# An expert stage fed by a weight stream: units of four experts moved ahead of the units of two, early loads by halves, and the last unit's products split by a branch

## The chip, the cores and the metric

The kernel runs on one core of a Trainium2 chip. The metric is the device time of one launch in microseconds (us). Before the change the median of 3 runs is 766.7 us (766.11 to 768.42). For this kernel, a difference within about 0.3% (2.3 us) can't be told from none.

## The reference

One layer of a hybrid encoder block on 256 tokens of width 1024, batch 1, in f32:

```
mod = silu(c) @ w_ada + b_ada                      # shift, scale, gate, twice
h   = rms_norm(x) * (1 + scale1) + shift1
... = h @ w_in                                     # two token mixers: neighbourhood and latent attention
x   = x + gate1 * (merged @ w_out)
h2  = rms_norm(x) * (1 + scale2) + shift2
scores = sigmoid(h2 @ w_router)                    # 64 experts, the best 8 of each token, group-limited
a   = silu(h2 @ w_gate[e]) * (h2 @ w_up[e]) * gate[token, e]
x   = x + gate2 * (sum over e of a @ w_down[e] + shared expert)
```

Each of the 64 experts has a gate and an up matrix of 1024 x 256 and a down matrix of 256 x 1024, so 3 MB in f32. Every expert's weights are read from HBM once: some 200 MB, most of what the kernel moves.

## The kernel before

The first 290 us or so are the two token mixers and the router. What the change touches is the expert stage behind them.

**Ranks and units.** The router counts the tokens of each expert, and the kernel sorts the experts by that count on the chip. The sorted places are called ranks. A *unit* is a group of experts that is computed together in 128 columns: two experts with 64 token slots each, two with 96 and 32, or four with 32 each (`UNITS`, L45 to L48). There are 26 units; `SEQ` is the order in which the ranks are loaded and used, and the units use up 64 experts in that order. I write U0, U1, ... U25 for the units in the order in which they run. Before the change U0 to U2 are units of two, and then come three units of two and one of four, again and again: the units of four are U6, U10, U14, U18, U22 and U25.

**Slots.** The weights live in six slots `Sl` (gate and up, 2 MB each) and six slots `Dl` (down, 1 MB each; in the rows one of them is called bias_t, and S and D stand for the others). The expert that is loaded into a slot is the one six places later in `SEQ`, so a unit's loads can only start when the unit that used those slots is through with them: `load_gu` (L790) when the products with gate and up are done, `load_dn` (L794) when the products with down are done. All of these loads are issued by SyncE (SP), in program order. An expert's number is itself read from a table in SBUF by SP (L774).

**A unit on TensorE (PE).** `middle(U)` computes the products with gate and up for k = 0 to 7 (`gate_up`, L1192), and between them, for the unit before, the products that add its result to the tokens (`last`, which calls `combine`: L1244 and L1245, with an add on VectorE, L1246). Behind `middle` come the unit's SiLU (L1213, L1214), the slot matrix (L1201), a part of the gather of tokens for units to come (L1179), the transposes (L1218) and the products with down (L1226), whose results are scaled and split in two (L1231 to L1233). The four or two experts of a unit stand beside each other in the columns of the array, so that a unit of four has as much work on PE as a unit of two, and twice the weights.

**The branch.** `past_slots` (L1281, L1282) holds a branch: if some expert had more tokens than its slots, extra passes are made. PE, VectorE, ScalarE and SyncE each read the largest overflow from SBUF into a register and branch on it; with the given inputs all four jump over the body. It stands in `middle` of the last unit, U25, behind the `last` of U24 and ahead of U25's own products.

**The tail.** Behind the products of U25 come its SiLU, transposes and down products, then `last_out` and the final adds, and four stores of the result (L1453).

Of the kernel before, what the change touches and what calls it, by code (L numbers as in the profile page):

```python
# [24 lines left out]
KD = D // P  # L25
# [16 lines left out]
TWOS = [((r, r + 54), (96, 32)) for r in range(6, 10)] + [((r, r + 1), (64, 64)) for r in range(10, 36, 2)]  # L42
FOURS = [(tuple(range(r, r + 4)), (32,) * 4) for r in range(36, 60, 4)]

UNITS = [((r, r + 1), (64, 64)) for r in (0, 2, 4)]  # L45
for u in FOURS:
    UNITS += TWOS[:3] + [u]
    del TWOS[:3]  # L48
SEQ = [r for u in UNITS for r in u[0]]
NUN = len(UNITS)  # L50

# [18 lines left out]
def unit_at(U):  # L70

    return sum(len(u[0]) for u in UNITS[:U])
# [3 lines left out]
def kernel(ctx, tc, x, c, positions, w_ada, b_ada, g_norm1, w_in, g_na_q, g_na_k,  # L76
# [710 lines left out]
    def load_gu(i, js=(0, 1), ks=slice(0, 8)):  # L787
        if i <= E:
            for j in js:
                Y.dma_start(gu_w(i)[:, j, ks], weights(i)[j].rearrange("(p k) f -> p k f", k=KD)[:, ks])  # L790

    def load_dn(i):
        if i <= E:
            Y.dma_start(dn_w(i), weights(i)[2].rearrange("(j p) d -> p j d" if i == 0 else "(p j) d -> p j d", j=2))  # L794
# [95 lines left out]
    for b in range(KD):  # L890
        u = 10 + b // 2
# [240 lines left out]
    def unit_slot(U):  # L1132

        return U % 4, U % 2
# [49 lines left out]
    def group_dst(g):  # L1184
        s = 2 * (g % 2)
        return lambda k: xg[:, s:s + 2, k]

    def gate_up(p, slot, U, ks, at=None):
        at = unit_at(U) + 1 if at is None else at
        for k in ks:  # L1190
            for c, w, i, _ in unit_tiles(U):
                T.matmul(p[c:c + w], xg[:, slot, k, c:c + w], gu_w(at + i)[:, :, k],  # L1192
                         start=(k == 0), stop=(k == KD - 1))
# [18 lines left out]
    def act(p):  # L1212
        A.activation(a_, p[:, 0:FF], AF.Silu)  # L1213
        V.tensor_tensor(a_, a_, p[:, FF:2 * FF], op=ALU.mult)  # L1214

    def a_trans():
        for j in range(2):
            T.transpose(b_mi[:, j * 128:(j + 1) * 128], a_[:, j::2], ident)  # L1218
        V.tensor_copy(aT.rearrange("p j n -> p (j n)"), b_mi[:, :256])  # L1219

    def down_mm(U, hf, at=None):
        at = unit_at(U) + 1 if at is None else at
        p = r_yy()
        for j in range(2):
            for c, w, i, _ in unit_tiles(U):
                T.matmul(p[c:c + w], aT[:, j, c:c + w], dn_w(at + i)[:, j, hf * 512:hf * 512 + 512],  # L1226
                         start=(j == 0), stop=(j == 1))
        return p
# [6 lines left out]
    def down(U, side, at=None):  # L1235
        for hf in range(2):
            down_out(down_mm(U, hf, at), hf, side)

    def combine(side, t, hfs=range(2)):
        so = so_t(side, t)  # L1240
        for hf in hfs:
            n_ = slice(hf * 512, hf * 512 + 512)
            p = r_co()
            T.matmul(p, so, yHt[:, hf], start=True, stop=False)  # L1244
            T.matmul(p, so, yLt[:, hf], start=False, stop=True)  # L1245
            V.tensor_tensor(X[:, t, n_], X[:, t, n_], p, op=ALU.add)  # L1246
# [19 lines left out]
    def past_slots():  # L1266


        on = [ENG.PE, ENG.DVE, ENG.Activation, ENG.SP]

        def load(i, r):
            if r < NS:
                w = w_exp_gate[0, r], w_exp_up[0, r], w_exp_down[0, r]
            else:
                v = nc.values_load(ordi[0:1, r - NS:r - NS + 1], min_val=0, max_val=E - 1, engines=[ENG.SP])
                w = [w_[0, bass.ds(v, 1)].rearrange("o a b -> (o a) b") for w_ in (w_exp_gate, w_exp_up, w_exp_down)]
            for j in range(2):
                Y.dma_start(gu_w(i)[:, j], w[j].rearrange("(p k) f -> p k f", k=KD))
            Y.dma_start(dn_w(i), w[2].rearrange("(p j) d -> p j d", j=2))

        most = nc.values_load(cmax[0:1, E // 2:E // 2 + 1], min_val=0, max_val=S, engines=on)  # L1281
        with tc.If(most > 0):  # L1282
            for j, U in enumerate(PAIRS):
                nv = nc.values_load(cmax[0:1, j:j + 1], min_val=0, max_val=S, engines=on)
                with tc.If(nv > 0):
                    for i, r in enumerate(UNITS[U][0]):
                        load(free_at + i, r)
                    cap = CAPS[2 * j]
                    extra(U, cap)
                    with tc.If(nv > 64):  # L1290
                        for first in range(cap + 64, S, 64):
                            extra(U, first)
# [3 lines left out]
    def last_out(pd):  # L1296

        down_out(pd[0], 0, 1)
        V.scalar_tensor_tensor(yB, pd[1], gsl2[1], gate2[:, 512:], op0=ALU.mult, op1=ALU.mult)

    def middle(U, early=lambda: None, also=lambda: None):

        gu = lambda ks: gate_up(b_gu, unit_slot(U)[0], U, ks)
        g, r = U // 2, U % 2
        oh_n = oh2[(g + 1) % 2]

        def last(t):
            if U:
                combine((U - 1) % 2, t)

        if U + 1 == NUN:
            for t in range(NT):
                last(t)
            past_slots()
            gu(range(KD))
            act(b_gu)
            a_trans()
            last_out([down_mm(U, hf) for hf in range(2)])
            return
        gu(range(0, 2))  # L1320
        early()
        if r == 0 and g + 1 < NGRP:
            for z in range(2):
                one_hot(oh_n, U + 2 + z)
        gu(range(2, 3))
        last(0)
        gu(range(3, 5))
        last(1)
        gu(range(5, 8))
        also()  # L1330
# [86 lines left out]
    for U in range(NUN):  # L1417
        g, r = U // 2, U % 2
        more = g + 1 < NGRP
        oh_n = oh2[(g + 1) % 2]  # L1420
        middle(U, *([] if U else [by_ranks, first_side]))
        if U + 1 == NUN:
            break

        nxt = [unit_at(U) + i + 1 + NS for i in range(len(UNITS[U][0]))]
        for ks in ((slice(0, 4), slice(4, 8)) if U == 0 else (slice(0, 8),)):
            for i in nxt:
                load_gu(i, ks=ks)
        act(b_gu)
        if U == 0:  # L1430
            for t in range(NT):
                shared_down(t)
            load_dn(NS)
        slot_side(oh2[(U + 1) // 2 % 2], U + 1, (U + 1) % 2)
        pg = [gather_mm(oh_n, 0, 4, 2 * r)] if more else []
        a_trans()
        if more:
            pg.append(gather_mm(oh_n, 0, 4, 2 * r + 1))
        for i, p in enumerate(pg):
            gather(oh_n, 0, 4, group_dst(g + 1), 2 * r + i, p)  # L1440
        down(U, U % 2)
        for i in nxt:
            load_dn(i)
# [32 lines left out]
```

## Time and profile before

| what | value |
|---|---|
| median of 3 runs | 766.7 us |
| the profiled execution's own time | 766.27 us |
| its span, first to last instruction | 764.6 us |
| TensorE (PE) busy | 707.4 us, 93% of the span |
| VectorE (DVE) busy | 394.8 us, 52% |
| ScalarE (ACT) busy | 221.2 us, 29% |
| GpSimd (POOL) busy | 12.2 us, 2% |
| mean granted TensorE clock | 0.957 |
| moved by DMA | 259.92 MB, mean 340 GB/s |

The busy share of PE counts matmuls that are slowed by the low clock as fully busy, and most of a matmul's time in the expert stage is the streaming of weights through the array. The span is 1.7 us shorter than the execution's own time. The expert stage starts at about 286 us of the span (the first products of L1192) and goes on to its end.

### The profile page before, as it was taken

The numbers are of one execution on the slowest core, as the hardware profiler recorded it, in microseconds if no ns is written. First come the engines' busy times: TensorE is split into PE (matmuls) and PEld (weight loads), VectorE is DVE, ScalarE is ACT, GpSimd is POOL, SyncE is SP. The second block draws the span as 40 slices with busy tenths as digits, with TensorE's granted clock in tenths as the row PEclk, the third lists the DMA queues.
The fourth block names the chain that finished last, engine by engine and source line by source line (L and its number), as shares of the span: only waits on it lengthen the run. The fifth ranks groups of instructions, "written<-read, shape, count | busy, mean of one in ns | idle before, by whom it ended". The sixth has DMA issues, their size and how long they took to land. (4 is left out here: it accounts for less than half of the span.)

```text
span 764.6 us, 12045 instructions
## 1 busy us (share of the span) xinstructions
PE 707.4 (93%) x4577; PEld 416.4 (54%) x4577; DVE 394.8 (52%) x942; ACT 221.2 (29%) x423; POOL 12.2 (2%) x52
## 2 busy tenths in 40 slices
PE   5998999999999999999999979996999699959957
PEld 4886968788799984444444423441445144514423
DVE  4555786545587487555555434542455244424422
ACT  3334474546654532111221111121112112201200
POOL 5000000000000100000000000000000000000000
PEclk9999998999999999999999989997999799979969
DMA  9999953745877967799999999999999999999981
GB/s 281 351 365 317 272 166 111 238 149 165 293 256 285 354 259 266 305 407 401 393 387 423 420 421 420 422 420 420 421 421 421 420 421 420 421 421 421 420 368 57
DMA packets 82347, 259.92 MB, mean 340 GB/s; under 512 B 5197, under 2 KB 54375, under 8 KB 57961
## 3 DMA queue, kind: packets, MB, share of 16 engines
q1 hardware_dynamic: 77204, 254.32, 86.0%
q10 hardware_dynamic: 4628, 4.74, 1.9%
q8 instruction: 38, 0.62, 0.3%
q14 instruction: 29, 0.23, 0.1%
q0 software_dynamic: 448, 0.02, 0.1%
HBM read 258.00 MB, written 1.05 MB: 339 GB/s over the span
## 5 line engine op out<-in xcount | busy, mean ns | idle before, releaser
L1192 PE MATMUL B<-S,xg 128*32 128x512 f32 (+1 forms) x1152 | 217.2, 638 | 33.5 <-DMA S<-in_w_exp_up_dram 27.2
L1192 PEld LDWEIGHTS B<-S,xg 128*32 128x32 f32 (+1 forms) x1152 | 60.1, 126 | 158.0 <-issue 138.5
L1246 DVE TENSOR_TENSOR X<-X,B 128x512 f32<-128x512 f32 x102 | 65.6, 683 | 94.8 <-PE B L1245 94.8
L1226 PE MATMUL B<-D,bias_t 128*32 128x512 f32 (+1 forms) x488 | 94.9, 597 | 1.1 <-DVE bias_t L1219 1.1
L1213 ACT ACTIVATE bias_t<-B 128x256 f32<-128x256 f32 x26 | 10.0, 386 | 249.3 <-PE B L1192 249.3
L1231 DVE SCALAR_TENSOR_TENSOR bias_t<-B,bias_t,gate 128x512 f32<-128x512 f32 x51 | 38.3, 750 | 38.8 <-PE B L1226 36.2
L1232 ACT CAST yHt<-bias_t 128x512 fp32r<-128x512 f32 x51 | 31.5, 617 | 84.9 <-DVE bias_t L1231 84.9
L1179 PE MATMUL B<-oh,xnH 128*128 128x256 f32 x208 | 53.8, 292 | 0.4 <-ACT xg L1167 0.4
L1226 PEld LDWEIGHTS B<-D,bias_t 128*32 128x32 f32 (+1 forms) x488 | 26.8, 121 | 49.3 <-issue 43.6
L1233 DVE TENSOR_TENSOR yLt<-bias_t,yHt 128x512 fp32r<-128x512 f32 x51 | 35.3, 692 | 34.9 <-ACT yHt L1232 34.9
L1179 PE MATMUL B<-oh,xnL 128*128 128x256 f32 x208 | 51.7, 281 | 0.0
L1214 DVE TENSOR_TENSOR bias_t<-bias_t,B 128x256 f32<-128x256 f32 x26 | 10.9, 421 | 73.1 <-ACT bias_t L1213 73.1
L408 DVE TENSOR_TENSOR Rw<-D,Rw 128x1024 fp32r<-128x1024 f32 x34 | 40.8, 1221 | 13.8 <-ACT Rw L403 13.6
L1244 PE MATMUL B<-yHt,so 128*128 128x512 f32 x102 | 46.2, 453 | 1.1 <-ACT yHt L1232 1.0
L1244 PEld LDWEIGHTS B<-yHt,so 128*128 128x128 f32 x102 | 19.3, 189 | 47.9 <-issue 20.8
L1167 ACT ACTIVATE xg<-B,sh,G 128x256 f32<-128x256 f32 x52 | 29.0, 564 | 52.7 <-PE B L1179 41.5
L1245 PE MATMUL B<-yLt,so 128*128 128x512 f32 x102 | 41.0, 402 | 0.4 <-DVE yLt L1233 0.2
L1226 PE MATMUL B<-bias_t 128*64 128x512 f32 (+1 forms) x88 | 40.0, 597 | 0.0
L1179 PEld LDWEIGHTS B<-oh,xnH 128*128 128x128 f32 x208 | 39.5, 190 | 0.6 <-ACT xg L1167 0.6
L119 PE MATMUL B<-Rh,Rw 128*128 128x256 f32 x128 | 39.6, 309 | 0.0
L1179 PEld LDWEIGHTS B<-oh,xnL 128*128 128x128 f32 x208 | 39.3, 189 | 0.2 <-DVE xnL L1335 0.2
L120 PE MATMUL B<-Rh,Rw 128*128 128x256 f32 x128 | 37.1, 290 | 0.0
(365 smaller groups left out, 1154.3 us busy)
## 6 DMA issues: line engine op xcount, KB each, us to landing
S<-in_w_exp_up_dram SPq DMA_DIRECT2D x62, 1024.0 KB, 19.8
S<-in_w_exp_gate_dram SPq DMA_DIRECT2D x62, 1024.0 KB, 15.3
D<-in_w_exp_down_dram SPq DMA_DIRECT2D x53, 1024.0 KB, 19.7
S<-in_w_ada_dram SPq DMA_DIRECT2D x20, 1024.0 KB, 8.5
bias_t<-in_w_exp_down_dram SPq DMA_DIRECT2D x11, 1024.0 KB, 19.7
D<-in_w_in_dram SPq DMA_DIRECT2D x6, 1024.0 KB, 13.4
S<-in_w_ada_dram SPq DMA_DIRECT2D x8, 512.0 KB, 7.3
D<-in_w_in_dram SPq DMA_DIRECT2D x8, 512.0 KB, 8.4
```

Of the source, the lines that this page charges most:

```text
L119: T.matmul(p, a[0], b[0], start=first, stop=False)
L120: T.matmul(p, a[0], b[1], start=False, stop=False)
L408: V.tensor_tensor(w_st[u][:, 1, z_], Dl[u % 2][:, z_], w_st[u][:, 0, z_], op=ALU.subtract)
L1179: T.matmul(p[:, k2 * 256:k2 * 256 + w], part[:, t, k], oh[:, t, c0:c0 + n].rearrange("p a b -> p (a b)"), start=(i == 0), stop=(i == 3))
L1192: T.matmul(p[c:c + w], xg[:, slot, k, c:c + w], gu_w(at + i)[:, :, k], start=(k == 0), stop=(k == KD - 1))
L1226: T.matmul(p[c:c + w], aT[:, j, c:c + w], dn_w(at + i)[:, j, hf * 512:hf * 512 + 512], start=(j == 0), stop=(j == 1))
L1231: V.scalar_tensor_tensor(yF, p, gsl2[side], gate2[:, hf * 512:hf * 512 + 512], op0=ALU.mult, op1=ALU.mult)
L1232: A.copy(yHt[:, hf], yF)
L1233: V.tensor_tensor(yLt[:, hf], yF, yHt[:, hf], op=ALU.subtract)
L1244: T.matmul(p, so, yHt[:, hf], start=True, stop=False)
L1245: T.matmul(p, so, yLt[:, hf], start=False, stop=True)
L1246: V.tensor_tensor(X[:, t, n_], X[:, t, n_], p, op=ALU.add)
```

## The change

Three edits. `UNITS` is built in another order: behind U0 to U2 each unit of four now stands ahead of three units of two, so the units of four are U3, U7, U11, U15, U19 and, as before, U25; in between U19 and U25 there are five units of two. The condition under which the loads behind a unit are issued by halves of k (first k = 0 to 3 of all its experts, then k = 4 to 7) is `U < 3 or U + 2 == NUN` in place of `U == 0`; NUN is 26. And in `middle` of the last unit the products for k = 0 to 3 stand ahead of the `last` of the unit before and of the branch.

```diff
@@ -43,9 +43,9 @@
 UNITS = [((r, r + 1), (64, 64)) for r in (0, 2, 4)]
-for u in FOURS:
-    UNITS += TWOS[:3] + [u]
-    del TWOS[:3]
+for i in range(5):
+    UNITS += [FOURS[i]] + TWOS[3 * i:3 * i + 3]
+UNITS += TWOS[15:] + FOURS[5:]
@@ -1309,10 +1309,11 @@
         if U + 1 == NUN:
+            gu(range(0, 4))
             for t in range(NT):
                 last(t)
             past_slots()
-            gu(range(KD))
+            gu(range(4, KD))
             act(b_gu)
@@ -1423,7 +1424,7 @@
         nxt = [unit_at(U) + i + 1 + NS for i in range(len(UNITS[U][0]))]
-        for ks in ((slice(0, 4), slice(4, 8)) if U == 0 else (slice(0, 8),)):
+        for ks in ((slice(0, 4), slice(4, 8)) if U < 3 or U + 2 == NUN else (slice(0, 8),)):
             for i in nxt:
                 load_gu(i, ks=ks)
```

**First place: the load queue of SP behind U1.** S_68 and S_70 are the slots of U1's two experts, and what is loaded into them are the two experts six places later. A row with 128x2048 is a whole matrix, 128x1024 a half; ISA rows set up the issue. The difference:

```order
+L790 DMA S_68<-in_w_exp_gate_dram 128x1024
+L790 ISA
+L790 DMA S_68<-in_w_exp_up_dram 128x1024
+L774 TENSOR_LOAD bias_t
+L774 ISA x2
+L790 ISA
+L790 DMA S_70<-in_w_exp_gate_dram 128x1024
+L790 ISA
+L790 DMA S_70<-in_w_exp_up_dram 128x1024
```

The first halves of both experts come first and the second halves behind them, and ahead of the down loads as before. Behind U2 the same is found; behind U3 and all later units the loads are of 128x2048 again.

**Second place: the products of U3 on PE.** S3, S0, S2 and S4 are slots of gate and up weights, B2 is the accumulator, xg the gathered tokens; the waits name DMA semaphores. Before:

```order
L1192 MATMUL B2_81<-S3_69,xg_2455 32x512 [waits DMAHW7_49,Activation_49]
L1192 MATMUL B2_81<-S3_69,xg_2455 32x512 x2
L1192 MATMUL B2_81<-S0_66,xg_2455 32x512 [waits DMAHW1_49,DMAHW0_49]
L1192 MATMUL B2_81<-S3_69,xg_2455 32x512 x3
L1192 MATMUL B2_81<-S0_66,xg_2455 32x512
```

And now:

```order
L1192 MATMUL B2_81<-S3_69,xg_2455 32x512 [waits DMAHW7_49,Activation_49]
L1192 MATMUL B2_81<-S0_66,xg_2455 32x512 [waits DMAHW1_49,DMAHW0_49]
L1192 MATMUL B2_81<-S2_68,xg_2455 32x512 [waits DMAHW2_49,DMAHW1_49]
L1192 MATMUL B2_81<-S4_70,xg_2455 32x512 [waits DMAHW4_49,DMAHW3_49]
L1192 MATMUL B2_81<-S3_69,xg_2455 32x512
```

There are four products to a k in both. Before, three of them read one slot and the fourth another; now they read four slots, so that U3 sets free four slots in place of two.

**Third place: PE around the branch of the last unit.** so0 is the slot matrix of U24, yHt and yLt its result. Before, from the last product with down of U24 on; the four products of a k of U25 come behind the branch:

```order
L1226 MATMUL B5_84<-D2_73,bias_t_75 64x512
L1244 MATMUL B7_86<-yHt_2460,so0_2458 128x512 [waits Activation_49]
L1245 MATMUL B7_86<-yLt_2461,so0_2458 128x512 [waits DVE_49]
L1244 MATMUL B6_85<-yHt_2460,so0_2458 128x512 [waits Activation_49]
L1245 MATMUL B6_85<-yLt_2461,so0_2458 128x512 [waits DVE_49]
L1244 MATMUL B7_86<-yHt_2460,so0_2458 128x512 [waits DVE_49]
L1245 MATMUL B7_86<-yLt_2461,so0_2458 128x512
L1244 MATMUL B6_85<-yHt_2460,so0_2458 128x512 [waits DVE_49]
L1245 MATMUL B6_85<-yLt_2461,so0_2458 128x512
```

Now the first products of U25 follow on the same last product of U24, with their waits for the loads of all four experts:

```order
L1226 MATMUL B5_84<-D2_73,bias_t_75 64x512
L1192 MATMUL B2_81<-S3_69,xg_2455 32x512 [waits DMAHW6_49,DMAHW5_49,Activation_49]
L1192 MATMUL B2_81<-S0_66,xg_2455 32x512 [waits DMAHW7_49,DMAHW0_49]
L1192 MATMUL B2_81<-S2_68,xg_2455 32x512 [waits DMAHW4_49,DMAHW3_49]
L1192 MATMUL B2_81<-S4_70,xg_2455 32x512 [waits DMAHW6_49,DMAHW5_49]
L1192 MATMUL B2_81<-S3_69,xg_2455 32x512
```

The sixteen products of k = 0 to 3 now stand ahead of the eight products L1244 and L1245, and these still directly ahead of the register load L1281 and the branch L1282. On SP, the last loads of the program (of two experts, four rows of 128x2048 and two downs, issued behind U23) stand as before and are whole: U24, to which `U + 2 == NUN` points, has no expert left to load.

## Rows read from the trace of the kernel before

**Rows 1.** The page of the profile: the span, the time of the engines, and the GB/s moved in each of 40 slices of 19.1 us.

```profile
span 764.6 us, 12045 instructions
PE 707.4 (93%) x4577; PEld 416.4 (54%) x4577; DVE 394.8 (52%) x942; ACT 221.2 (29%) x423; POOL 12.2 (2%) x52
GB/s 281 351 365 317 272 166 111 238 149 165 293 256 285 354 259 266 305 407 401 393 387 423 420 421 420 422 420 420 421 421 421 420 421 420 421 421 421 420 368 57
```

**Rows 2.** Stretches of the expert stage: from:to, length, busy us of PE, PEld, DVE, ACT, POOL with instructions, granted clock, busy share of the DMA engines, GB/s.

```profile
308.00:316.50 8.50, 8.50 (x40) 3.12 (x38) 4.56 (x7) 0.62 (x1) 0.00 (x0) 1.00 0.74 282
316.50:319.50 3.00, 3.00 (x23) 2.19 (x20) 1.03 (x4) 0.76 (x2) 0.00 (x0) 1.00 0.20 57
319.50:332.00 12.50, 12.50 (x57) 4.76 (x58) 8.08 (x27) 2.36 (x4) 0.00 (x0) 1.00 1.01 426
332.00:336.00 4.00, 4.00 (x28) 2.78 (x26) 2.19 (x8) 1.05 (x3) 0.00 (x0) 1.00 0.88 334
336.00:349.00 13.00, 13.00 (x90) 4.27 (x87) 5.70 (x9) 2.21 (x5) 0.00 (x0) 1.00 1.01 423
349.00:352.00 3.00, 3.00 (x28) 2.43 (x31) 2.42 (x8) 1.21 (x4) 0.00 (x0) 1.00 0.85 295
352.00:365.00 13.00, 13.00 (x106) 4.63 (x99) 6.76 (x19) 2.36 (x5) 0.00 (x0) 1.00 1.01 421
365.00:370.00 5.00, 5.00 (x48) 2.74 (x51) 2.99 (x9) 1.69 (x4) 0.00 (x0) 1.00 0.93 356
380.00:385.00 5.00, 5.00 (x48) 3.07 (x51) 3.08 (x9) 1.81 (x4) 0.00 (x0) 1.00 0.94 344
395.00:400.00 5.00, 5.00 (x44) 3.11 (x44) 2.51 (x9) 1.82 (x4) 0.00 (x0) 1.00 0.95 328
406.00:736.00 330.00, 299.69 (x1568) 125.17 (x1560) 144.16 (x295) 54.62 (x106) 0.00 (x0) 0.94 1.01 421
```

**Rows 3.** The load queue of SP in order of time, 305 to 352 us: start, us, line, what is loaded.

```profile
317.53 0.34 SPq L790 DMA_DIRECT2D S<-in_w_exp_gate_dram  x1
...
333.11 0.33 SPq L790 DMA_DIRECT2D S<-in_w_exp_gate_dram  x1
...
348.82 0.33 SPq L790 DMA_DIRECT2D S<-in_w_exp_gate_dram  x1
```

**Rows 4.** What SP waited for in its queue, 305 to 352 us: in total, times, longest.

```profile
SPq L790 <- PE B L1192: 23.3, 3, 7.9
SPq L794 <- PE B L1226: 11.9, 3, 5.4
```

**Rows 5.** The last loads of SP, 713 to 726 us, as in rows 3.

```profile
713.51 0.33 SPq L790 DMA_DIRECT2D S<-in_w_exp_gate_dram  x1
...
725.96 0.33 SPq L794 DMA_DIRECT2D bias_t<-in_w_exp_down_dram  x1
```

**Rows 6.** The instructions of the branch's line, by queue: SP's last wait is the landing of the last up matrix; a wait behind the branch is the first thing an engine does after it.

```profile
L1282 SPq EVENT_SEMAPHORE  x7: 17/17/17, 732.5 to 741.4; - x7
L1282 ACTq EVENT_SEMAPHORE  x2: 17/17/17, 737.5 to 737.6; - x2
L1282 PEldq EVENT_SEMAPHORE  x2: 51/51/51, 741.3 to 741.5; - x2
L1282 DVEq EVENT_SEMAPHORE  x2: 21/21/21, 742.0 to 742.1; - x2
L1282 SPq COMPARE_BRANCH  x1: 53/53/53, 727.2 to 727.2; - x1
L1282 ACTq COMPARE_BRANCH  x1: 58/58/58, 732.3 to 732.3; - x1
L1282 PEldq COMPARE_BRANCH  x1: 6126/6126/6126, 735.2 to 735.2; - x1
L1282 DVEq COMPARE_BRANCH  x1: 72/72/72, 736.4 to 736.4; - x1
```

**Rows 7.** PE in order of time at the end: the last of the `last` of U24, and the products of U25 (64 rows).

```profile
734.75 0.63 PE L1245 MATMUL B<-yLt,so 128*128 128x512 f32 x1
741.74 10.01 PE L1192 MATMUL B<-S,xg 128*32 128x512 f32 x64 [6.37 <-PEq L1282]
```

**Rows 8.** The end in stretches, cut where the granted clock changes (columns as in rows 2).

```profile
733.60:741.70 8.10, 1.78 (x4) 0.71 (x4) 1.86 (x3) 0.00 (x0) 0.00 (x0) 0.50 1.00 409
741.70:747.30 5.60, 5.56 (x28) 4.12 (x32) 0.00 (x0) 0.00 (x0) 0.00 (x0) 0.50 0.30 120
747.30:751.80 4.50, 4.45 (x42) 2.76 (x34) 0.00 (x0) 0.00 (x0) 0.00 (x0) 1.00 0.00 0
```

**Rows 9.** PE in order of time in the products of U1: the rows of k = 0 to 2, of the `last` of U0, and of k = 3 and 4 (four rows to a k in the trace).

```profile
307.93 2.74 PE L1192 MATMUL B<-S,xg 128*64 128x512 f32 x12
310.60 0.50 PE L1244 MATMUL B<-yHt,so 128*128 128x512 f32 x1
...
311.73 1.94 PE L1192 MATMUL B<-S,xg 128*64 128x512 f32 x8
```

**Rows 10.** The stretch in which the loads behind U0 flow, which are by halves already before the change (columns as in rows 2).

```profile
297.00:308.00 11.00, 11.00 (x50) 5.71 (x51) 7.98 (x15) 2.01 (x4) 0.00 (x0) 1.00 0.98 373
```

**Rows 11.** The page's group of the adds behind `combine`: count, busy us, mean ns of one, idle time before them.

```profile
L1246 DVE TENSOR_TENSOR X<-X,B 128x512 f32<-128x512 f32 x102 | 65.6, 683 | 94.8 <-PE B L1245 94.8
```

**Rows 12.** The stores of the result, which go out when the load queue is empty: KB each, median us from issue to landing.

```profile
out_dram<-X SPq DMA_DIRECT2D x2, 256.0 KB, 2.1
```

**Rows 13.** PE in the products of a unit of four that waits for its loads (U18).

```profile
595.62 1.05 PE L1192 MATMUL B<-S,xg 128*32 128x512 f32 x4
600.22 1.57 PE L1192 MATMUL B<-S,xg 128*32 128x512 f32 x2 [3.54 <-DMA S<-in_w_exp_up_dram]
```

**Rows 14.** The granted clock around that wait (columns as in rows 2).

```profile
594.00:600.50 6.50, 2.96 (x13) 0.57 (x10) 3.69 (x8) 1.24 (x2) 0.00 (x0) 1.00 1.01 421
600.50:610.80 10.30, 7.00 (x21) 1.41 (x20) 0.00 (x0) 0.00 (x0) 0.00 (x0) 0.50 1.01 419
```

**Rows 15.** PE in order of time in the down products of U25, the first and the last row.

```profile
753.76 0.63 PE L1226 MATMUL B<-D,bias_t 128*32 128x512 f32 x3 [0.52 <-DVE bias_t L1219]
...
756.80 0.59 PE L1226 MATMUL B<-bias_t 128*32 128x512 f32 x1
```

## The prediction

> **What bounds the kernel now.** I read the page first: PE is busy for 93% of the span, but the GB/s line stands at 420 to 421 from the 22nd slice to the 37th, and at 387 to 407 in the four slices ahead of that [rows 1]. PE's share also holds the time in which the low clock draws its products out (below), so I asked which of the two sets the end. The stretches answer it [rows 2]. From 308 to 400 us PE is busy without a break (each stretch has as much busy time as length) and the weight stream has holes: here PE is the bound, and the load queue shows why, since a load waits for the products that still read its slot (23.3 us in three waits for L1192, 11.9 us for L1226) [rows 3, 4]. From 406 to 736 us the stream runs at 421 GB/s and PE is busy for only 299.69 of 330 us: here the stream is the bound, and what was lost in the holes before 400 is never made up.
>
> The end: the last loads are issued from 713.51 to 725.96 [rows 5], and SP sees the last up matrix land at 741.4 [rows 6]. PE takes the branch at 735.2 and is held in it for 6126 ns, until 741.3 [rows 6]; U25's products begin at 741.74 [rows 7]. So the stall in the branch and the stream end together: today the branch costs 0.3 us at most, because PE would have waited for the weights. The 64 rows of products take 10.0 us [rows 7]: the first 5.6 us at the low clock level (28 rows, 1.2 GHz), the other 36 rows at full clock (2.4 GHz) in 4.4 us [rows 8].
>
> **The change part by part.**
>
> *Halves behind U1 and U2.* They let a load start when k = 0 to 3 are done. U1's products begin at 307.93, k = 3 is the first half of the eight rows at 311.73, so the first halves can be issued at about 312.7 in place of 317.53 [rows 3, 9]. The hole at 308 to 320 closes. How fast halves flow is seen behind U0: 373 GB/s against 421 to 426 for whole matrices [rows 2, 10]. Follow the queue from 316.6 us, where the downs behind U0 are through (282 GB/s up to 316.5, then 57 [rows 2]): gate and up of two experts are 4.19 MB, 11.2 us at 373; their downs 2.1 MB, 4.9 us at 426. Behind U1: 327.8 and 332.8; behind U2: 344.0 and 348.9. The next load can't start before U3's products are done, and these end where they did: SP issues at 348.82 [rows 3], because PE is busy throughout and nothing of its work up to there gets shorter. Before, the stream came to that point with its queue still draining (295 GB/s from 349 to 352); now it is empty by 348.9, a moment later it starts again. So the halves gain next to nothing: what they pull forward is waited away at U3. I take 0, with 0 to 0.9 us as bounds (0.9 is the hole at 349 to 352: 3 us x (1 - 295/421)).
>
> The Trainium skill, "DMA: Bandwidth & Descriptors", section "Bandwidth", asks for transfers of at least 1 MiB; the halves are of 512 KB, and rows 10 agree in kind (373 against 421). By its 341 GB/s for 1 MiB as the rate of a half, an estimate, U2's downs would be through at 351 and not at 348.9, and 2 us of U3's loads would come late; the sum here goes by 373.
>
> *A unit of four as U3.* It sets free four slots at 348.8 where a unit of two freed two: 12.6 MB, 29.9 us of stream, so that U4's and U5's slots are free long before the queue runs dry. The three later holes close: 5 us x (1 - 356/421) = 0.8, 5 x (1 - 344/421) = 0.9, 5 x (1 - 328/421) = 1.1 [rows 2], together 2.8 us. From there the stream runs at 421 to its end. The five units of two in a row at the end don't starve it: one takes PE some 15.6 us (U1 to U2: 317.53 to 333.11 at the same place [rows 3]) and 6.3 MB are 14.9 us, and the four slots of U19 give a lead of 15 us, of which five units use 0.7 us each. So the last up matrix lands 2.8 us sooner, at 738.6. Bounds: 0 (a new hole elsewhere) and 3.7 (with the 0.9 above).
>
> *Halves behind U24.* Nothing: U24 has no expert to load, and the order shows SP's last loads whole. U25's products for k = 0 need all four experts, so they start when the stream is through, at about 738.8.
>
> *Half of the products ahead of the branch.* Now the 32 rows of k = 0 to 3, the `last` of U24 and the branch stand in one line behind the last landing. Before, the second and third were under the stream. Counted from the start of the products:
> - 32 rows: PE comes from a longer idle time than before, so the low clock as before, 28 rows in 5.6 us, and 4 at full clock 0.5: 6.1 us.
> - Eight products L1244 and L1245: four of them take 1.13 us (310.60 to 311.73 [rows 9]), the other four wait for adds of 683 ns to free the two banks [rows 11]. With the second pair behind the first add: 2.6 us.
> - Register load and branch: 0.4 us behind the start of the last product (734.75 to 735.2 [rows 6, 7]).
> - The stall in the branch. All four engines have it: SP 5.3 (727.2 to 732.5), ACT 5.2, DVE 5.6, PE 6.1 us [rows 6], all under a full stream. When PE gets there now, at about 748, the stream is over. No row shows the stall with an empty queue. From below: a store with an empty queue takes 2.1 us from issue to landing [rows 12]; from above 6.1. The nearest rows are the four stalls themselves; I take 5.0, a little under the shortest.
> - From the stall's end to the first product, 0.5 us (741.3 to 741.74 [rows 6, 7]).
> - The other 32 rows. At full clock 3.9 us (36 rows in 4.4). But PE has then idled over 5 us, and 3.54 us of idling at U18 ended with the clock at 0.50 for the next 10.3 us [rows 13, 14]. So I take the low level again, 28 rows in 5.6 us and 4 in 0.5: 6.1 us.
>
> Together 6.1 + 2.6 + 0.4 + 5.0 + 0.5 + 6.1 = 20.7 us where there were 10.0: 10.7 us more. VectorE's branch comes 0.7 us behind PE's and its stall lies beside PE's and the second half. Behind the products the tail is as before. The start was 0.3 us behind the landing, now 0.2.
>
> The Trainium skill, "Runtime: NRT & Kernel Launch", section "Instruction fetch mechanics", says that a taken branch to a page not held makes the sequencer fetch it by DMA before it goes on. By that rule the fetch begins when the branch is taken and can't lie beside the products ahead of it, which speaks against rival C below; rows 6 agree with a stall of this kind on each engine.
>
> *Sum.* -2.8 (stream) - 0.1 (start) + 10.7 (tail) = +7.8 us. Against the execution's own 766.27 us (span 764.6) that is 774.1; the median is 0.4 above that execution, so 774.5; I say 774.
>
> **The rivals.**
> - A. A short stall and a clock that holds: 2.1 us, and the second half at 3.9. The tail is 15.6 us, +5.6; with -2.9 it is +2.7: 769.4. For it: the queue is empty. Against: four stalls of 5.2 us and more, and the clock at U18.
> - B. The clock stays low behind the products too. The down products run from 753.8 to 757.4 at full clock [rows 15], and would take 3.6 us more: 778. For it: the tail's idle gaps; against: the clock held through the same gaps before (full from 747.3 on [rows 8], and these products are at full speed).
> - C. The stall is hidden: PE's sequencer takes the branch while the products run. Tail 6.1 + 2.6 + 0.5 + 3.9 = 13.1, +3.1, with -2.9: 767. Against: the last four products wait for adds on VectorE, and the branch stands behind them.
> - D. Faster: the holes from 308 to 352 are won as well: 2.8 + 2.6 + 0.8 + 0.9 = 7.1 us by the same sum (282, 57, 334 and 295 GB/s [rows 2]), so 9.9 with the later ones, and the tail is rival A's. 766.7 - 9.9 - 0.1 + 5.6 = 762. It decides where U3's products end: they would have to end some 7 us sooner than 348.8. PE's full stretches speak against it.
>
> **How the numbers follow.** The forecast 0.50, A 0.18, B 0.13, C 0.11, D 0.08. A difference under 0.3% (2.3 us, to 764.4 and 769.0) can't be told from none. Faster is D: 0.08. The same is C and some of A: 0.19. Slower is the rest: 0.73. The range goes from 767.5 (D and part of C left out below) to 778.5 (B with the longest stall left out above); the bounds of the stall alone, 2.1 to 6.1, make 771 to 775.
>
> **What would show it.** In the profile after: 421 GB/s without holes from about 352 us, and a hole just before; PE's first products of U3 at 339 and the load behind them at 348.8, as before; the first product of U25 at 738.5 to 739.5; PE's branch at about 748 and a stall of 4 to 6 us in it; a granted clock of 0.50 behind it; the span from the first to the last product of U25 about 20 us. I am wrong if the first product of U25 comes before 736 (rival D), or if the products' span is under 16 us (A, C).

## The result, and the profile after

Over five runs each on one chip the changed kernel takes 773.11 us (772.79 to 775.57) and the kernel before 768.28 us (766.11 to 769.72): a ratio of 1.0079, 95% interval 1.006 to 1.0098, or 4.6 to 7.5 us slower. The forecast was 774.0 us, +7.8 us: the sign and the mechanism are right, the size is a little high. That 774.0 and 773.11 lie so close is in part luck: the forecast started from a median of 766.7 us, and with two more runs the kernel before has 768.28.

The profiled execution of the changed kernel took 775.57 us, the slowest of its five. Against the one before (766.27 us) it is 9.3 us longer, and three differences make that up. Its expert stage began 1.8 us later (first product of U0 at 288.44 us, before at 286.64), ahead of every load and product that was moved. From there to the landing of the last up matrix it took 740.8 - 288.44 = 452.4 us, before 454.8: 2.4 us less. From the landing to the end of U25's products it took 20.2 us, before 10.35: 9.9 us more. The first products of U0, before and now:

```profile
286.64 1.94 PE L1192 MATMUL B<-S,xg 128*64 128x512 f32 x8
```

```profile
288.44 1.94 PE L1192 MATMUL B<-S,xg 128*64 128x512 f32 x8
```

The page's span, engine and GB/s lines, which answer to [rows 1]:

```profile
span 773.9 us, 12074 instructions
PE 710.0 (92%) x4577; PEld 415.4 (54%) x4577; DVE 394.6 (51%) x942; ACT 221.2 (29%) x423; POOL 12.4 (2%) x52
GB/s 279 353 363 306 264 164 110 242 140 163 300 243 308 343 241 304 349 416 348 421 420 420 420 422 421 420 422 419 422 420 422 419 422 421 420 420 420 421 146 56
```

Where 407, 401, 393 and 387 stood in the 18th to 21st slices there is now one dip, 348 in the 19th, and then 420 to the end of the stream. The same in stretches, cut as in [rows 2], whose columns they have:

```profile
308.00:316.50 8.50, 8.50 (x38) 3.12 (x34) 4.51 (x7) 1.24 (x2) 0.00 (x0) 1.00 0.90 360
316.50:319.50 3.00, 3.00 (x15) 1.03 (x15) 0.94 (x2) 0.12 (x1) 0.00 (x0) 1.00 0.94 244
319.50:332.00 12.50, 12.50 (x64) 5.93 (x63) 8.10 (x29) 3.01 (x6) 0.00 (x0) 1.00 1.01 395
...
336.00:349.00 13.00, 13.00 (x89) 5.17 (x91) 7.28 (x14) 2.36 (x4) 0.00 (x0) 1.00 1.00 405
349.00:352.00 3.00, 3.00 (x29) 1.75 (x21) 0.82 (x5) 0.70 (x2) 0.00 (x0) 1.00 0.09 30
352.00:365.00 13.00, 13.00 (x106) 4.97 (x109) 8.15 (x22) 2.36 (x4) 0.00 (x0) 1.00 0.99 414
365.00:400.00 35.00, 35.00 (x284) 15.91 (x280) 18.96 (x50) 7.14 (x15) 0.00 (x0) 1.00 1.01 421
400.00:736.00 336.00, 301.36 (x1629) 127.72 (x1622) 145.75 (x297) 56.78 (x110) 0.00 (x0) 0.94 1.01 421
```

The holes at 308 to 320 are partly filled (360 and 244 GB/s for 282 and 57), and the three between 365 and 400 are gone. In their place is one, 30 GB/s from 349 to 352. SP's load queue shows what makes it; the rows answer to [rows 3]:

```profile
314.63 0.33 SPq L790 DMA_DIRECT2D S<-in_w_exp_gate_dram  x1
...
341.07 1.84 SPq L794 DMA_DIRECT2D D<-in_w_exp_down_dram  x2
350.59 0.33 SPq L790 DMA_DIRECT2D S<-in_w_exp_gate_dram  x1
```

The first half behind U1 goes out at 314.63 in place of 317.53, and this in a run that is 1.8 us late. But after the downs at 341.07 nothing can be issued until U3's products are done: 350.59, which less the 1.8 us is the 348.8 of before.

At the end, the branch's line by queue, which answers to [rows 6], and PE's waits of the register load ahead of it:

```profile
L1282 SPq EVENT_SEMAPHORE  x7: 17/17/17, 731.0 to 740.8; - x7
...
L1282 DVEq EVENT_SEMAPHORE  x2: 21/21/21, 754.1 to 754.2; - x2
L1282 PEldq EVENT_SEMAPHORE  x2: 51/51/51, 754.3 to 754.4; - x2
...
L1282 PEldq COMPARE_BRANCH  x1: 3826/3826/3826, 750.4 to 750.4; - x1
L1282 DVEq COMPARE_BRANCH  x1: 72/72/72, 751.2 to 751.2; - x1
```

```profile
L1281 PEldq EVENT_SEMAPHORE  x4: 51/51/51, 749.4 to 749.7; - x4
```

PE in order of time there, which answers to [rows 7]:

```profile
729.13 1.05 PE L1192 MATMUL B<-S,xg 128*32 128x512 f32 x4
735.99 1.89 PE L1192 MATMUL B<-S,xg 128*32 128x512 f32 x2 [5.81 <-SPq L1282]
740.95 6.41 PE L1192 MATMUL B<-S,xg 128*32 128x512 f32 x26 [3.07 <-SPq L1282]
747.29 0.50 PE L1244 MATMUL B<-yHt,so 128*128 128x512 f32 x1
...
748.80 0.50 PE L1244 MATMUL B<-yHt,so 128*128 128x512 f32 x1 [0.32 <-DVE X L1246]
...
749.73 0.40 PE L1245 MATMUL B<-yLt,so 128*128 128x512 f32 x1
754.55 6.46 PE L1192 MATMUL B<-S,xg 128*32 128x512 f32 x32 [4.42 <-PEq L1282]
```

And the stretches cut at the changes of the granted clock, as in [rows 8] (0.50 and 0.51 are the low level, 1.2 GHz):

```profile
740.90:746.60 5.70, 5.65 (x25) 1.48 (x26) 0.00 (x0) 0.00 (x0) 0.00 (x0) 0.50 0.24 99
746.60:753.40 6.80, 3.21 (x10) 1.27 (x8) 2.57 (x4) 0.00 (x0) 0.00 (x0) 1.00 0.01 4
753.40:760.30 6.90, 5.75 (x28) 1.57 (x32) 0.00 (x0) 0.00 (x0) 0.00 (x0) 0.51 0.01 4
760.30:768.00 7.70, 6.06 (x46) 2.05 (x39) 3.13 (x6) 1.00 (x2) 0.00 (x0) 1.00 0.01 2
```

Between the 26 and the 32 rows lie the `last` of U24 (747.29 to about 750.1, with a wait for VectorE's add at 748.80), the branch at 750.4, 3.83 us in it, and then 28 rows at half the clock. DVE takes its branch at 751.2 and goes on at 754.1: 2.9 us, beside PE's.

### The profile page after: what moved, and what is told of

Its sections match the earlier page's. It is cut to its first block, busy times and chain, and to the rows that moved or that the text cites. A ratio compares the mean times of both kernels' runs of the same rounds, so it can differ in the third digit from the quotient of the medians.

```text
span 773.9 us, 12074 instructions
## 1 busy us (share of the span) xinstructions
PE 710.0 (92%) x4577; PEld 415.4 (54%) x4577; DVE 394.6 (51%) x942; ACT 221.2 (29%) x423; POOL 12.4 (2%) x52
## 5 line engine op out<-in xcount | busy, mean ns | idle before, releaser
L1192 PE MATMUL B<-S,xg 128*32 128x512 f32 (+1 forms) x1152 | 220.1, 644 | 41.0 <-DMA S<-in_w_exp_up_dram 27.7
L1192 PEld LDWEIGHTS B<-S,xg 128*32 128x32 f32 (+1 forms) x1152 | 57.3, 127 | 172.2 <-issue 157.5
L1244 PE MATMUL B<-yHt,so 128*128 128x512 f32 x102 | 45.6, 447 | 0.3 <-DVE X L1246 0.3
L1244 PEld LDWEIGHTS B<-yHt,so 128*128 128x128 f32 x102 | 19.1, 187 | 44.5 <-issue 17.6
L1245 PE MATMUL B<-yLt,so 128*128 128x512 f32 x102 | 40.4, 396 | 0.1
L1226 PE MATMUL B<-bias_t 128*32 128x512 f32 (+1 forms) x88 | 40.0, 597 | 0.0
```

## The experiments

The theory after the result: the third edit alone loses, since the wait in the branch, which lay under the stream, now stands behind it; the units of four win some 2 us, the halves next to nothing. The first rival: the units cost what they win, and the tail costs less than the trace shows. The second rival concerns the tail: it is not the branch that costs but the split of the products, or the `last` of U24 standing in the middle of them.

### Each edit alone

**The first two edits without the third.** Against the changed kernel:

```diff
-            gu(range(0, 4))
             for t in range(NT):
                 last(t)
             past_slots()
-            gu(range(4, KD))
+            gu(range(KD))
```

> The changed kernel with its third edit undone: all products of U25 stand behind the branch again; units and halves as changed. Theory (the unit of four as U3 wins 2 to 3 us of the weight stream, and the split of the last products costs about 10 us): 2 to 3 us faster than before, ratio about 0.9965; PE's stall in the branch again about 6 us, ending with the stream. Rival (the new order of units or the later start of the expert stage costs too, and the split costs only some 5 us): 0 to 2 us slower than before.

Measured: 766.17 us against 768.22, ratio 0.9977 (0.9958 to 0.9997).

**The third edit alone**, on the kernel before:

```diff
+            gu(range(0, 4))
             for t in range(NT):
                 last(t)
             past_slots()
-            gu(range(KD))
+            gu(range(4, KD))
```

> The kernel before with the third edit alone. Theory: 9 to 10 us slower than before, ratio 1.012 to 1.013, with the first product for k=0 of all four experts right behind the last landing, a stall of 3.8 us in the branch and the low clock behind it; about 20 us from the last landing to the end of U25's products. Rival (split costs some 5 us, the rest of the difference lies ahead of it): 4 to 6 us slower.

Measured: 776.98 us against 768.22, ratio 1.0137 (1.0108 to 1.0166), 8.3 to 12.8 us slower. The term of the forecast was 10.6. PE's stall is 3612 ns in this run, and the products end 18.6 us behind the landing, 8.2 us later than before and 1.6 us sooner than in the changed kernel: the second half took 4.93 us here, 6.46 there.

**The first edit alone:** `UNITS` of the changed kernel in the kernel before, loads and tail as they were.

```diff
-for u in FOURS:
-    UNITS += TWOS[:3] + [u]
-    del TWOS[:3]
+for i in range(5):
+    UNITS += [FOURS[i]] + TWOS[3 * i:3 * i + 3]
+UNITS += TWOS[15:] + FOURS[5:]
```

> The first edit alone: units of four ahead of three units of two, loads by halves behind U0 only, products of U25 behind the branch. Theory (what halves pull forward is waited away at U3): within 1 us of the kernel with units and halves. Rival (the halves close a hole that counts): 2 to 3 us slower than that one, so as slow as before.

Measured: 766.51 us, ratio 0.9986 (0.9967 to 1.0006). With the halves it was 0.9977: the intervals lie over one another, and by the traces the way from U0's first product to the landing is 452.8 us with the halves and 453.2 without, before 454.8. So by the traces the halves up to U2 are worth 0.4 us and the units 1.6. The runs are less sharp: they can't tell the first edit alone from no change, and they leave room for more by the halves. In the trace of the first edit alone (an execution of 771.12 us, the slowest of its twelve) PE takes the branch at 739.7 and comes out at 746.0, 2.1 us after the landing at 743.9: where the stream ends sooner against PE's work, the cover of the branch grows thin.

### The hole at 349 to 352

If the products of U3 make it, halves behind U3 as well must close it, since the first halves then need only k = 0 to 3 of U3. On the kernel without the third edit:

```diff
-        for ks in (... if U < 3 or U + 2 == NUN else (slice(0, 8),)):
+        for ks in (... if U < 4 else (slice(0, 8),)):
```

> Units as changed, products of U25 behind the branch, loads by halves behind U0 to U3 in place of U0 to U2. Theory (the hole at 349 to 352 us, 2.3 us by the landings, is the wait for the end of U3's products): the loads behind U3 start some 4.8 us sooner, the hole closes, and with 8 MB by halves at some 3% less speed (0.6 us) it is 1.5 to 2 us faster than with halves behind U0 to U2, 4 to 5 us faster than before. Rival (the smaller transfers cost what they win): the same as with halves behind U0 to U2.

Measured: 763.59 us against 768.22, ratio 0.9941 (0.9917 to 0.9965), 2.6 us better than with halves up to U2. The stretches, first of the kernel with halves up to U2, then with halves up to U3:

```profile
345.00:349.00 4.00, 4.00 (x36) 1.36 (x30) 1.28 (x2) 0.00 (x0) 0.00 (x0) 1.00 0.79 330
349.00:353.00 4.00, 4.00 (x36) 2.72 (x32) 2.38 (x8) 1.30 (x4) 0.00 (x0) 1.00 0.54 178
```

```profile
345.00:349.00 4.00, 4.00 (x32) 1.35 (x28) 1.56 (x3) 0.00 (x0) 0.00 (x0) 1.00 0.99 412
349.00:353.00 4.00, 4.00 (x36) 2.72 (x32) 2.12 (x8) 0.95 (x3) 0.00 (x0) 1.00 1.02 405
```

The hole is gone, PE's work in these stretches is the same, and the landing comes 451.3 us behind U0's first product, 1.5 sooner. So the hole was U3's products, and the two edits left it half used: what halves pull forward behind U0 to U2 is kept only if U3 gives its slots back early too. Halves up to U3 in the old order of units were not run, so how much of this hangs on the first edit is not shown. A new wait stands behind it. PE in order of time, and the branch, in this kernel:

```profile
740.85 9.08 PE L1192 MATMUL B<-S,xg 128*32 128x512 f32 x64 [7.03 <-PEq L1282]
```

```profile
L1282 PEldq COMPARE_BRANCH  x1: 6252/6252/6252, 734.1 to 734.1; - x1
```

The landing is at 739.3, and PE comes out of the branch at 740.4: 1.1 us are waited there.

### What in the tail costs

**Halves at the unit that has something to load.** `U + 2 == NUN` points to U24, which loads nothing. At U23 stand the loads of the last two experts. On the changed kernel:

```diff
-        for ks in (... if U < 3 or U + 2 == NUN else (slice(0, 8),)):
+        for ks in (... if U < 3 or U + 3 == NUN else (slice(0, 8),)):
```

> The changed kernel with its second condition pointed at U23, the unit behind which the last loads are really issued: the last two experts come by halves, the products of U25 are split by the branch as changed. Theory (the cost is the line of half the products, the last of U24, the stall and the other half behind the last landing): the first half now starts some 5 us ahead of the last landing, the line is as long as before but begins earlier, so 5 to 6 us faster than the changed kernel, 0 to 3 us slower than before. Rival (PE waits for something else than the loads): no faster than the changed kernel.

Measured: 768.19 us against 767.8, ratio 1.0015 (0.9994 to 1.0036); the changed kernel had 1.0079. PE in order of time:

```profile
734.36 6.08 PE L1192 MATMUL B<-S,xg 128*32 128x512 f32 x26 [1.41 <-DMA S<-in_w_exp_up_dram]
...
747.31 6.57 PE L1192 MATMUL B<-S,xg 128*32 128x512 f32 x32 [4.09 <-PEq L1282]
```

The first half now runs under the stream (the landing is at 740.3), some 6 us sooner. The `last`, 3.47 us of stall and the slow second half stay behind it, and that is enough to use up what the stream gained.

**Without the branch.** On the changed kernel:

```diff
                 last(t)
-            past_slots()
             gu(range(4, KD))
```

> The changed kernel without the branch and its body (the passes for overflowing experts are left out; with the given inputs none is taken). Theory (stall 3.8 us, register load and return about 1 us, low clock in the second half 2.5 us): 7 to 8 us faster than the changed kernel, the products of U25 end some 13 us behind the last landing without a second stretch of low clock; 1 to 2 us faster than before. Rival (the split itself, with the last of U24 in between, is what costs): 2 to 3 us faster than the changed kernel at most.

Measured: 766.83 us against 767.8, ratio 0.9986 (0.9967 to 1.0006). PE in order of time:

```profile
739.15 5.18 PE L1192 MATMUL B<-S,xg 128*32 128x512 f32 x26 [3.95 <-DMA S<-in_w_exp_up_dram]
...
747.04 3.64 PE L1192 MATMUL B<-S,xg 128*32 128x512 f32 x32
```

The products end 11.5 us after the 26 rows began (739.15 to 750.68), in the changed kernel 20.1 (740.95 to 761.01). The 8.6 us between are the 4.42 us in which the products waited for the branch, 2.8 us of the second half, which without that idle time runs at full clock (3.64 for 6.46 us), and 1.2 us of the first half, which left the low clock sooner. So of the 8.6 some 7 hang on the branch. What the split and the place of `last` cost beside it is small: the products' 11.5 us stand against 10.0 [rows 7].

**The `last` of U24 ahead of the products.** The three steps stay ahead of the branch, in another order:

```diff
-            gu(range(0, 4))
             for t in range(NT):
                 last(t)
+            gu(range(0, 4))
             past_slots()
             gu(range(4, KD))
```

> The changed kernel with the last of U24 put ahead of the first half of the products again; the branch still splits them. Theory: the eight products L1244 and L1245 go back under the stream, 2 to 3 us faster than the changed kernel, 3 to 4 us slower than before; PE's stall in the branch, behind the end of the stream, 3.6 to 4.5 us, with the low clock behind it. Rival (these products cost nothing, they lie beside the register load and the branch of VectorE): as slow as the changed kernel.

Measured: 765.46 us against 767.8, ratio 0.9971 (0.9956 to 0.9986). This expectation fell, and with it a part of the theory: a branch behind products was held to cost its stall wherever they stand. PE in order of time, and PE's sequencer at the waits of the register load and at the branch:

```profile
742.41 5.89 PE L1192 MATMUL B<-S,xg 128*32 128x512 f32 x26 [3.95 <-SPq L1282]
748.60 3.64 PE L1192 MATMUL B<-S,xg 128*32 128x512 f32 x32 [0.30 <-PEq L1282]
```

```profile
L1281 PEldq EVENT_SEMAPHORE  x4: 51/51/51, 742.5 to 742.8; - x4
...
L1282 PEldq COMPARE_BRANCH  x1: 3566/3566/3566, 743.5 to 743.5; - x1
```

The waits of the register load, which stand behind the 26 rows in the program, begin at 742.5: 0.1 us after the first of the rows began, with most of them still to run. PE's sequencer had handed them on and gone ahead. The branch's 3.57 us (743.5 to 747.1) lie beside the rows, which end at 748.30, and the second half follows 0.30 us behind them at full clock. So it is the order within the three steps that costs: in the changed kernel the last pairs L1244 wait for VectorE's adds (the 0.32 us at 748.80), and while the sequencer waits it hands nothing on. It comes to the register load only when the last pair starts (749.39, the waits at 749.4), and to the branch at 750.4.

**All products ahead of the branch**, with the `last` first; how far does the sequencer go ahead?

```diff
-            gu(range(0, 4))
             for t in range(NT):
                 last(t)
+            gu(range(KD))
             past_slots()
-            gu(range(4, KD))
```

> The changed kernel with the last of U24 first, then all products of U25, then the branch. New theory, from the run with the last first (PE takes the branch while queued products still run, unless a product that waits for VectorE stands ahead of it): the branch is taken some us after the last landing with products still running, its stall lies beside them, and the time is within 2 us of that run, 1 to 3 us faster than before; how long after the first product the branch is taken tells how far PE's queue runs ahead. Old theory (the branch waits for the products): the stall of 3.6 us and the low clock stand behind the products, 3 to 6 us slower than before.

Measured: 768.4 us against 768.38, ratio 1.0004 (0.9979 to 1.0028): as fast as before the change, which neither expectation had. The waits and the branch, and PE with the products and the first down products:

```profile
L1281 PEldq EVENT_SEMAPHORE  x4: 51/51/51, 747.4 to 747.7; - x4
...
L1282 PEldq COMPARE_BRANCH  x1: 3687/3687/3687, 748.4 to 748.4; - x1
```

```profile
742.17 8.72 PE L1192 MATMUL B<-S,xg 128*32 128x512 f32 x58 [3.95 <-SPq L1282]
753.14 0.70 PE L1218 MATMUL B<-idg,bias_t 128*128 128x128 f32 x2 [2.25 <-DVE bias_t L1214]
754.36 1.07 PE L1226 MATMUL B<-D,bias_t 128*32 128x512 f32 x3 [0.52 <-DVE bias_t L1219]
```

The products are the shortest of all from the landing (742.1 to 750.9, 8.8 us), but the sequencer came to the waits of the register load at 747.4 with 22 of the 64 rows still to start, and left the branch at 752.1, after the products' end at 750.9. ScalarE's SiLU of U25 had to wait for PE's L1282 too: it began at 752.25, 1.4 us behind the products' end, where in the changed kernel it was 0.1 us (761.13 behind 761.01). Down products take 1.07 us where [rows 15] have 0.63: the granted clock is 0.50 from 753.05 to 759.90.

The queue covers a stall only for as long as what is in it lasts. In the kernel with 32 rows ahead of the branch four of the 26 rows had started when the sequencer came by at 742.5, and again 22 were left. The difference is how long these 22 took. The stretches, first of that kernel and then of the one with all products ahead (columns as in [rows 2]):

```profile
742.40:748.30 5.90, 5.89 (x26) 1.39 (x26) 0.00 (x0) 0.00 (x0) 0.00 (x0) 0.61 0.24 94
```

```profile
747.00:753.05 6.05, 3.90 (x34) 1.04 (x25) 0.38 (x1) 0.38 (x1) 0.00 (x0) 1.00 0.02 5
```

At a mean clock of 0.61 they lasted 5.8 us from the waits on, and the stall was over after 4.6. At full clock they lasted 3.5 us, and the stall was over after 4.7. So part of what made the kernel with the `last` first look free is that its rows were slow.

**The two versions that should win.** First halves up to U3 and at U23 with all products behind the branch, as before the change; against the first two edits:

```diff
-        for ks in (... if U < 3 or U + 2 == NUN else (slice(0, 8),)):
+        for ks in (... if U < 4 or U + 3 == NUN else (slice(0, 8),)):
```

> Units as changed, halves behind U0 to U3 and behind U23, all products of U25 behind the branch. Theory (PE leaves the branch only when the last matrix has landed, so that earlier halves find it still in the stall): within 1.5 us of the same kernel without the halves behind U23, 4 to 6 us faster than before. Rival (the landing of the last two matrices sets the start of the products): 3 to 5 us faster than that kernel, 8 to 10 us faster than before.

Measured: 764.52 us against 767.8, ratio 0.996 (0.9931 to 0.9988): no gain over the 0.9941 without the halves at U23, as the theory had it. What lands sooner finds PE in the branch until 739.4, and the landing is at 739.5. Then the same halves with the `last` first and the products of k = 0 to 3 ahead of the branch:

```diff
-            gu(range(0, 4))
             for t in range(NT):
                 last(t)
+            gu(range(0, 4))
             past_slots()
...
-        for ks in (... if U < 3 or U + 2 == NUN else (slice(0, 8),)):
+        for ks in (... if U < 4 or U + 3 == NUN else (slice(0, 8),)):
```

> Units as changed, halves behind U0 to U3 and behind U23, the last of U24 ahead of the first half of U25's products, then the branch, then the other half. New theory (the stall lies beside the first half, and that half now starts 5 to 6 us ahead of the last landing): the branch is taken ahead of the last landing, PE is out of it about 1 us after, the second half runs at full clock, the products end some 5 us behind the last landing in place of 10; 8 to 10 us faster than before, ratio about 0.988. Old theory (the stall begins when the first half is done): the products end 12 us or more behind the landing, 2 to 4 us faster than before.

Measured: 763.59 us against 768.38, ratio 0.9936 (0.9908 to 0.9963): faster, by less than expected. PE in order of time, the branch, and the stretch of the low clock:

```profile
735.69 3.64 PE L1192 MATMUL B<-S,xg 128*32 128x512 f32 x32
743.90 6.60 PE L1192 MATMUL B<-S,xg 128*32 128x512 f32 x32 [4.58 <-PEq L1282]
```

```profile
L1282 PEldq COMPARE_BRANCH  x1: 5952/5952/5952, 737.6 to 737.6; - x1
```

```profile
742.80:749.60 6.80, 5.70 (x28) 3.20 (x32) 0.00 (x0) 0.00 (x0) 0.00 (x0) 0.50 0.05 18
```

The first half is through at 739.3, at full clock and under the stream. But the branch is taken while the stream still runs, and takes 5.95 us: until 743.6, 2.3 us after the landing at 741.3. Behind the idle 4.58 us the clock is at the low level, and the second half takes 6.60 us. The expectation had the short stall and the fast second half of the kernel with the `last` first.

The runs side by side. "Branch" and "end" are counted from the landing of the last up matrix (SP's last wait in the branch's line), the end being that of U25's products:

| kernel | time ratio | branch taken | stall, us | end |
|---|---|---|---|---|
| before | 1 | -6.2 | 6.13 | +10.4 |
| changed | 1.0079 | +9.6 | 3.83 | +20.2 |
| third edit alone | 1.0137 | +9.7 | 3.61 | +18.6 |
| without the third edit | 0.9977 | -6.7 | 6.01 | +9.6 |
| first edit alone | 0.9986 | -4.2 | 6.15 | +12.7 |
| halves up to U3, third undone | 0.9941 | -5.2 | 6.25 | +10.6 |
| changed, halves at U23 | 1.0015 | +3.2 | 3.47 | +13.6 |
| changed, `last` first | 0.9971 | +1.2 | 3.57 | +9.9 |
| `last` and all products first | 1.0004 | +6.3 | 3.69 | +8.8 |
| halves up to U3 and at U23, third undone | 0.996 | -6.1 | 5.97 | +8.9 |
| `last` first, halves up to U3 and at U23 | 0.9936 | -3.7 | 5.95 | +9.2 |

The best two, 0.9936 and 0.9941, can't be told apart; both beat the kernel before and the changed one. The first edit wins some 1.6 us by its trace, the second one has to reach one unit further, and the third one is to be left out, or kept with the `last` ahead of the products.

## Why the prediction was right, and what in it was not

**The stream, -2.8 us.** Right in place, nearly in size: -2.4 in the changed kernel's trace, -2.0 and -1.6 in those without the third edit and with the first alone. The holes closed where it said (414 and 421 GB/s from 352 on), and a new one came just before 352, with the cause that it gave. Two readings were off. The stretches with halves don't run at one rate: beside the 373 of [rows 10] stand 395 to 413 here, and 365 from 318 to 330 us in the kernel without the third edit, each time with the DMA engines fully busy (0.98 to 1.02); what sets the rate is open. The queue ran dry at about 349, which is 347 in the kernel before, sooner than at the 348.9 or 351 of the forecast, and the new hole is longer. And "what they pull forward is waited away at U3" was told as an end of the matter: it names the wait that one more step of halves takes away, for 2.6 us by the medians.

**The loads behind U24, nothing.** Right: nothing is loaded there.

**The tail, 20.7 us from the first product.** Measured from the 26 rows on: 20.1 (740.95 to 761.01). By terms, in the changed kernel:
- 32 rows 6.1: 26 rows from 740.95 to 747.29, 6.3 us. That all 64 rows wait for the last landing was wrong: of k = 0 the rows of three of the four experts ran at 729.13 and 735.99, as their weights came. So the mark "the first product of U25 before 736 would be rival D" was a bad one: it did come before, and D was not the case.
- `last` 2.6 and the way to the branch 0.4: 747.29 to 750.4, 3.1 us.
- The stall 5.0: 3.83. This is the term that was mis-sized. The four stalls of [rows 6], to which it was set, all lay under a full stream. Taken behind the landing PE's stall was 3.47 to 3.83 us in five kernels; taken ahead of it, 5.95 to 6.25 in six. The sign named for it, 4 to 6 us, was missed by 0.2.
- The return 0.5: 0.3.
- The second half 6.1, at the low clock: 6.46, at 0.51. The row of U18, from which this was drawn, was the right neighbour.

So the tail's total is nearer than its terms: the stall was taken 1.2 us too long, and the other terms together 0.5 us too short. VectorE's branch, put 0.7 us behind PE's though [rows 6] have 1.2, came 0.8 behind.

**Start, -0.1 us.** The 26 rows begin 0.15 us behind the landing, as taken.

**The sum, +7.8.** The traces give -2.4 + 9.9 = +7.5 between the two profiled executions, without the later start of the stage. Run against run it is 4.6 to 7.5. The two parts measured alone, +10.5 and -1.8 us (ratios 1.0137 and 0.9977 of 768.2), make +8.8; the changed kernel's interval ends below that, though those of the parts, 8.3 to 12.8 and -3.2 to -0.2, reach it. The traces put it the other way, some +5.3 by the parts (the third edit alone 8.2 - 0.1, the other two -2.0 - 0.8), so how well the parts add up stays open.

**The rivals.** A had a short stall and a clock that holds: the stall was between, the clock fell. B did not come: the down products behind were at full clock (6.06 us of PE at 1.00 from 760.3 on). D fell with PE's full stretches. C, the hidden stall, did not happen, and for the reason given: the last products wait for adds and the branch stands behind them. But the sentence on the Trainium skill went too far. The Trainium skill, "Runtime: NRT & Kernel Launch", section "Instruction fetch mechanics", says that a taken branch to a page not held waits for its fetch; it does not say that the branch is taken only when the products ahead of it have run. With the `last` first the stall of 3.57 us lay beside the rows and cost 0.3. The forecast had weighed what the four adds cost (1.5 us of 2.6) and not what they prevent (some 7 us, by the run without the branch).

## What to carry to other kernels

In these runs PE's sequencer handed matrix products on and went up to 22 rows ahead of them. A branch behind products without waits then cost 0.3 us where the rows in the queue lasted longer than register load and stall together (5.8 against 4.6 us), and not where they were shorter (3.5 against 4.7). One product that waited for another engine directly ahead of the branch held it back until the last pair ran. So put what waits first, the long run of products next and the branch behind it, with some of the products behind the branch, and check in the trace how long the queue lasts at the clock that is granted there. And where loads are split so as to start early, follow the queue to the next place where it must wait, and split there too: the gain is kept only from the last such place on.

## What was not expected of the hardware

The stall in the branch has two sizes, by whether the weight stream runs: on PE 3.47 to 3.83 us when it was taken behind the landing of the last up matrix, and 5.95 to 6.25 when it was taken ahead of it, under the stream; on DVE 2.9 in the changed kernel (751.2 to 754.1) and 5.6 before (736.4 to 742.0). The last down matrix can still be on its way in the first case: with the `last` first the branch was taken at 743.5, and 213 GB/s flowed until 744.0. That the stall and the stream share the DMA engines or the memory would explain it, but no run here takes them apart.

PE's sequencer ran ahead of the rows by 22, in both kernels with the `last` first that come to the branch behind the landing. Whether that is a fixed depth, and what sets it, was not tried.

A stall of 3.7 us at the end of the products, seen as 2.25 us of idling in front of L1218, was followed by 6.85 us at a granted clock of 0.50; 0.30 us of idling was not. The start of the expert stage, which no edit touches, moved between 286.6 and 290.7 us over the profiled executions of these kernels, and was at 288.6 with the third edit alone, which changes only the end; why is open.
